# A bidirectional mLSTM and convolution block on one core: projections in another order, and the scan's incoming weights made on ScalarE

## The chip, the core and the metric

The kernel runs on one core of a Trainium2 chip. The core has a matrix engine (TensorE; PE in the views, its weight loads PEld), VectorE (DVE), ScalarE (ACT), GpSimd (POOL) and SyncE (SP, which here only issues DMAs). Each engine works through its own instructions in the order in which the program holds them, and waits on semaphores for the others. The metric is the device time of one execution in microseconds. Before the change it is 2687.62 us, the median of three runs from 2687.34 to 2690.5.

## What is computed

One layer over 2048 latent tokens and 256 context tokens of width 1024. One input projection with 11,296 columns feeds a gated convolution and an mLSTM scan that runs in both directions over 8 heads. Both outputs are projected again, merged with sigmoid gates, projected out and added to the input. Cut to its core:

```python
hx = rmsnorm(x, g_norm[l]) * (1 + scale[:, None, :]) + shift[:, None, :]
px = hx @ w_in[l] + b_in[l]
h_ctx, ctx_states = mlstm_bidir(pc[..., :STATE_COLS], (zero_state(bsz), zero_state(bsz)), not last)
h_x, _ = mlstm_bidir(px[..., :STATE_COLS], ctx_states, True)
out_x = mixer_output(h_x, px[..., STATE_COLS:], True, ...)
x = x + gate[:, None, :] * out_x
# one step of the scan, per chunk
m_row = jnp.maximum(log_w.max(-1), log_inter)
s = jnp.einsum('bhid,bhjd->bhij', qc, kc) * jnp.exp(log_w - m_row[..., None])
w_inter = jnp.exp(log_inter - m_row)
num = jnp.einsum('bhij,bhje->bhie', s, vc) + w_inter[..., None] * jnp.einsum('bhid,bhde->bhie', qc, C)
C_new = decay[..., None, None] * C + jnp.einsum('bhj,bhjd,bhje->bhde', wk, kc, vc)
```

## The kernel before

**Halves and pairs.** The tokens are worked in two halves of 1024. For each half the input projection is cut into 44 "pairs" of 256 columns, named by a letter and a number 0 to 3: k, v, q are the scan's, o and z its output gates, X, C, Z, B the convolution's (X and C are multiplied and convolved, Z is the SiLU path, B the last factor), a and b the merge gates. `pair` (L396 on) makes each product with seven block products instead of eight ("ops" 0 to 6, banks X Y X W Z V Z), each of 12 matmuls of 512 columns (L412), so 84 a pair. The operands are split in a high and a low part: `split` (L177) has ScalarE cast the high part (`wh`, L178) and VectorE subtract the low part (`wl`, L179), which the third matmul of an op reads. `Stream` keeps the weight operands three ops ahead; GpSimd makes their sums (`sw`, L345).

**What follows a pair.** `half_fins` (from L883) holds what is done with a pair's four results. On VectorE three of them first get an addend (L874, or L881 together with the bias); then C costs one multiplication and two shifted multiply-adds each (L942, L947, L949), Z two operations each (L962, L963), z two (L927, L928), B one (L970), and o, a, b none. Bank Z is written by op 4, read by the addend of `fin(1, 1)` on VectorE, and written again by op 6: the matmuls of op 6 wait for that read.

**Side work.** Generators run beside the dense matmuls, some steps for each matmul: `prep_b` and `late_rows` prepare the second half's input and the output weights (1024 columns wide on VectorE, L205, L217, L295, L1289, L1312), `ctx_scan` and `state_scan` carry the states, `scan` makes the outputs. TensorE's order is that of the code (manual schedule). On the other engines a scheduler sets the order when the program is built; `pin` keeps marked instructions in program order there.

**The scan.** For every two chunks `load` (L753) fetches tokens `tk`, queries and keys `qk` and a tile `mw` with the row maxima and the incoming weights of both directions, read from the scratch `mwd` where `gate_finish` (L560) put them (`mr` and `wr`). `mask` (L776) has GpSimd fill the masked part of the maxima. `start` (L784) takes two exponentials on ScalarE (`wt`, L792), the score matmul, two VectorE products (`pt` L796, `qw` L799) and a weighted value tile `vw` (`weigh`, L628) on GpSimd. After it come the state update (L636, L640) and the output matmuls (L842, L843).

**Between the halves.** `xB.load` (L252) fetches the second half's operands into the slots of the first half's, as the last pair lets go of them (slots x0 to x27, four to each op), and splits them; then the gate weights `gw` (L473, L475) are loaded and split.

Of the kernel before, what the change touches and what calls it, by code (L numbers as in the profile page):

```python
# [41 lines left out]
def hybrid_kernel(ctx: ExitStack, tc, x, c, ctxt, c_ctx, w_ada, b_ada, g_norm, w_in, b_in,  # L42
# [425 lines left out]
    mwd = [dp.tile([64, 2, 2, P], F32, name=f"mwd{i}") for i in range(2)]  # L468
# [91 lines left out]
    def gate_finish(key, d, half):  # L560
        g = gt[key][d]
        n, nch = g["n"], g["nch"]
        mp = tp.tile([P, 8, nch], F32, tag="gtmp", name=nm("mp"), bufs=3)
# [17 lines left out]
        g.update(dec=dec, wk=wk)  # L581
# [46 lines left out]
    def weigh(tk, wk):  # L628

        vw = tp.tile([P, 129], F32, tag="vw", name=nm("vw"), bufs=3)  # L630
        pin(nc.gpsimd.tensor_scalar(vw, tk[:, VT], wk, None, op0=OP.mult))  # L631
        return vw
# [111 lines left out]
    def scan(pool, heads, half, done=None):  # L744
# [8 lines left out]
        def load(m):  # L753

            if m >= len(flat) // 2:
                return
# [4 lines left out]
            qks[m] = pool.tile([P, 2, 2, P], F32, tag="qk", name=nm("qk"), bufs=2)
            ld.dma_start(qks[m].rearrange("p a c i -> p a (c i)"), qkd[half][h, :, c0 // 2])
            mws[m] = pool.tile([P, 2, 2, 2, P], F32, tag="mw", name=nm("mw"), bufs=2)
            src = mwd[half]
            ld.dma_start(mws[m], bass.AP(tensor=src.tensor, offset=src.offset + (h * NC + c0) * 4 * P,
                                         ap=[[0, P], [4 * P, 2], [2 * P, 2], [P, 2], [1, P]]))
# [53 lines left out]
        start(0)  # L820
        yield
        due = []
        for n, (h, ch) in enumerate(flat):
            j = h * NC + ch
            if n % 2 == 0:
                load(n // 2 + 1)
            else:
                mask(n // 2 + 1)
# [15 lines left out]
            yield from gap(4)  # L844
# [636 lines left out]
    def begin(m, wait=0):  # L1481
# [4 lines left out]
        xts[m] = []  # L1486
        for i in range(2):
# [96 lines left out]
```

## Time and profile before

| what | us |
|---|---|
| median of the runs | 2687.62 |
| the profiled execution, whole | 2680.46 |
| its span in the trace | 2678.7 |
| TensorE busy | 2602.4 |
| VectorE busy | 1728.2 |
| GpSimd busy | 1151.2 |
| ScalarE busy | 1063.5 |

The profiled execution is one of its own, 7.2 us under the median. The span is what the trace shows; 1.8 us lie around it. A view of stretches of time ("windows") gives for each stretch the busy time of each engine, the granted TensorE clock as a share of full speed, and what the DMAs moved. The timeline lists instructions with their start, their duration and, in brackets, how long the engine stood idle before them and what ended that.

The first half's pairs k0 to v3 end at about 382 us, its other pairs run to about 1057 us, the second half's to about 2070 us, the four branch projections to 2507 us, the output projection to the end.

### The profile page before, as it was taken

The page shows a single profiled execution, that of the slowest core. Times are in us where ns is not written, and L with a number is a line of the kernel's source. Part 1 is how long each engine was busy: PE and PEld are TensorE (multiplying, and loading weights), DVE is VectorE, ACT ScalarE, POOL GpSimd, SP SyncE. Part 2 cuts the span into 40 slices and gives each one's busy share as a digit, 9 for nine tenths or more (in the row PEclk, how much of TensorE's full clock was granted, in tenths as well). Part 3 has the DMA queues.
Part 4 walks back from the last instruction along what each step waited for, and adds up shares of the span by engine and source line. Part 5 has one row for each costly group of instructions (what it writes and reads, how often), then busy time and mean ns, then how long its engine had stood idle before and what let it go on. Part 6 is the DMA issues. An engine that isn't in the chain of part 4 may idle for free.

```text
span 2678.7 us, 38162 instructions
## 1 busy us (share of the span) xinstructions
PE 2602.4 (97%) x12807; PEld 2172.9 (81%) x12807; DVE 1728.2 (65%) x3113; ACT 1063.5 (40%) x2170; POOL 1151.2 (43%) x1371
## 2 busy tenths in 40 slices
PE   7999999999999999999999999999999999999998
PEld 6788887787778887877887888888888888788777
DVE  5643238887876657478578577667666655554697
ACT  4533344333343435343443444344444433332333
POOL 2221223232345443235555564565655235432664
PEclk8999999999999999999999999999999999999999
DMA  7323343454643567424644654653566978868542
GB/s 222 105 92 109 101 150 122 158 180 144 214 145 100 174 178 238 128 91 146 205 151 117 205 159 126 191 174 128 157 193 210 304 238 259 286 195 284 202 164 95
DMA packets 370080, 458.09 MB, mean 171 GB/s; under 512 B 23852, under 2 KB 268252, under 8 KB 369884
## 3 DMA queue, kind: packets, MB, share of 16 engines
q1 hardware_dynamic: 369648, 455.57, 54.3%
q8 instruction: 102, 1.67, 0.3%
q14 instruction: 94, 0.77, 0.1%
q10 hardware_dynamic: 236, 0.08, 0.0%
HBM read 324.60 MB, written 130.97 MB: 170 GB/s over the span
## 4 chain that ended last, share of the span: by engine, by line
PE 82%; DVE 8%; issue 3%; DMA 3%; ACT 2%; POOL 2%; SPq 0%; ACTq 0%; POOLq 0%; DVEq 0%
PE pd L412 58%; PE pd L459 12%; PE pn L842 2%; PE pn L843 2%; PE pc L439 2%; DVE wl L179 2%; PE pn L636 1%; PE pa L647 1%; PE pa L794 1%; PE pu L636 1%; DVE cv L947 1%; PE pd L492 1%; DMA x<-xod 1%; DVE t2k L874 1%; DVE x L179 1%
## 5 line engine op out<-in xcount | busy, mean ns | idle before, releaser
L412 PE MATMUL pd<-x,wh 128*128 128x512 f32 x5320 | 1699.2, 398 | 18.2 <-DVE t2k L874 11.0
L412 PEld LDWEIGHTS pd<-x,wh 128*128 128x128 f32 x5320 | 986.8, 189 | 212.0 <-issue 23.8
L412 PE MATMUL pd<-x,wl 128*128 128x512 f32 x2660 | 1059.6, 398 | 0.0
L412 PEld LDWEIGHTS pd<-x,wl 128*128 128x128 f32 x2660 | 502.8, 189 | 99.3 <-issue 0.2
L178 ACT CAST wh<-sw 128x512 fp32r<-128x512 f32 x384 | 238.0, 620 | 506.2 <-PE pd L412 422.3
L179 DVE TENSOR_TENSOR wl<-sw,wh 128x512 fp32r<-128x512 f32 x384 | 314.9, 821 | 186.6 <-ACT wh L178 180.0
L178 ACT CAST wh<-wr 128x512 fp32r<-128x512 f32 x352 | 217.6, 619 | 404.7 <-PE pd L412 267.6
L345 POOL TENSOR_TENSOR sw<-wr,sw 128x512 f32<-128x512 f32 x96 | 136.5, 1422 | 455.7 <-DVE wl L179 404.0
L179 DVE TENSOR_TENSOR wl<-wr,wh 128x512 fp32r<-128x512 f32 x352 | 287.1, 816 | 47.7 <-ACT wh L178 46.7
L459 PE MATMUL pd<-x,wh 128*128 128x512 f32 x896 | 282.7, 397 | 0.0
L631 POOL TENSOR_SCALAR vw<-tk,wk 128x129 f32<-128x129 f32 x240 | 182.6, 765 | 151.5 <-PE pn L636 119.4
L345 POOL TENSOR_TENSOR sw<-wr 128x512 f32<-128x512 f32 x96 | 131.9, 1374 | 189.1 <-DVE wl L179 182.0
L459 PEld LDWEIGHTS pd<-x,wh 128*128 128x128 f32 x896 | 167.1, 189 | 32.2
L459 PE MATMUL pd<-x,wl 128*128 128x512 f32 x448 | 174.2, 399 | 0.0
L345 POOL TENSOR_TENSOR sw<-sw,wr 128x512 f32<-128x512 f32 x96 | 134.8, 1404 | 70.1 <-DVE wl L179 59.2
L874 DVE TENSOR_TENSOR t2k<-pd,u 128x512 f32<-128x512 f32 x168 | 115.5, 687 | 62.2 <-PE pd L412 60.7
L855 ACT ACTIVATE hf<-pn,rd 128x128 f32<-128x128 f32 x128 | 46.9, 366 | 273.1 <-DVE rd L851 254.3
L780 POOL TENSOR_SCALAR_AFFINE_SELECT mw<-mw 128x256 f32<-128x256 f32 x128 | 62.9, 511 | 205.3 <-DMA mw<-mwd 166.4
L345 POOL TENSOR_TENSOR sw<-wr,wr 128x512 f32<-128x512 f32 x96 | 135.7, 1413 | 17.2 <-DMA wr<-in_w_in_dram 7.8
L186 POOL TENSOR_SCALAR ssq<-ssq 128x1 f32<-128x1 f32 x128 | 36.3, 284 | 198.7 <-ACT hf L857 193.3
L842 PE MATMUL pn<-tk,pt 128*128 128x129 f32 x512 | 98.9, 275 | 4.7 <-DVE hb L856 4.7
L881 DVE SCALAR_TENSOR_TENSOR t2k<-pd,cols,u 128x512 f32<-128x512 f32 x73 | 54.7, 750 | 71.2 <-PE pd L412 68.4
(244 smaller groups left out, 3309.8 us busy)
## 6 DMA issues: line engine op xcount, KB each, us to landing
wr<-in_w_in_dram SPq DMA_DIRECT2D x176, 512.0 KB, 3.8
mw<-mwd SPq DMA_DIRECT2D x64, 512.0 KB, 4.9
tk<-tokd SPq DMA_DIRECT2D x64, 386.0 KB, 3.9
qkd<-t2k SPq DMA_DIRECT2D x64, 256.0 KB, 2.8
qk<-qkd SPq DMA_DIRECT2D x64, 256.0 KB, 4.1
tk<-tokd SPq DMA_DIRECT2D x48, 257.0 KB, 2.8
tokd<-t2k SPq DMA_DIRECT2D x32, 258.0 KB, 3.0
x<-in_w_ada_dram SPq DMA_DIRECT2D x16, 512.0 KB, 6.8
```

Source lines behind the costliest of these rows:

```text
L178: a = nc.scalar.copy(hi, raw)
L179: b = (eng or nc.vector).tensor_tensor(lo, raw, hi.bitcast(F32), op=OP.subtract)
L345: nc.gpsimd.tensor_tensor(s, a, b, op=op)
L412: nc.tensor.matmul(ps[b], op[wi][:, kk, :], xs.at(o, xi, kk), start=(fresh and kk + pi == 0), stop=(o == last[b] and kk == 3 and pi == 2), ...
L439: nc.tensor.matmul(cps[:, s], op[wi][:, kk, :], cx[ci][xi][:, kk, :], start=(first and kk + pi == 0), stop=(not first and kk == 3 and pi = ...
L459: nc.tensor.matmul(pss[j], ops[k // 4][wi][:, k % 4, :], y(xi, k, j), start=(k + pi == 0), stop=(k == NK - 1 and pi == 2))
L631: pin(nc.gpsimd.tensor_scalar(vw, tk[:, VT], wk, None, op0=OP.mult))
L636: nc.tensor.matmul(pu, tk[:, KT], vw, start=True, stop=True)
L780: pin(nc.gpsimd.affine_select(mws[m][:, :, 0, d, :], mws[m][:, :, 0, d, :], pattern=[[0, 2], [s, P]], base=0, channel_multiplier=-s, compa ...
L842: nc.tensor.matmul(pn[:, d, :], pt[:, d, :], tk[:, VT], start=True, stop=False)
L874: nc.vector.tensor_tensor(t, ps, add, op=OP.add)
L881: nc.vector.scalar_tensor_tensor(dst, ps, bcol(col), add, op0=OP.add, op1=OP.add)
```

## The change

Four things are changed: the order of the pairs in both halves, where the weights `wr` and the values `vw` are made, when `mw` and `qk` are fetched, and two small lengths (the wait after a fetch of the last branch's operands, 24 steps instead of 12, and one small tile for two in the output).

```diff
-    mwd = [dp.tile([64, 2, 2, P], F32, name=f"mwd{i}") for i in range(2)]
+    mwd = [dp.tile([64, 2, P], F32, name=f"mwd{i}") for i in range(2)]
...
-        wr = tp.tile([64, P], F32, tag="ar", name=nm("wr"), bufs=1)
-        nc.scalar.activation(wr, mr, AF.Exp, bias=mpc, scale=-1.0)
-        ld.dma_start(mwd[half][:, 0, d, :], mr)
-        ld.dma_start(mwd[half][:, 1, d, :], wr)
+        ld.dma_start(mwd[half][:, d, :], mr)
...
-        vw = tp.tile([P, 129], F32, tag="vw", name=nm("vw"), bufs=3)
-        pin(nc.gpsimd.tensor_scalar(vw, tk[:, VT], wk, None, op0=OP.mult))
+        vw = tp.tile([P, 129], F32, tag="vw", name=nm("vw"), bufs=2)
+        pin(nc.scalar.activation(vw, tk[:, VT], AF.Copy, scale=wk))
...
+        def load_rows(m):
...
+            mws[m] = pool.tile([P, 2, 2, 2, P], F32, tag="mw", name=nm("mw"), bufs=2)
+            src = mwd[half]
+            ld.dma_start(mws[m][:, :, 0], bass.AP(tensor=src.tensor, offset=src.offset + (h * NC + c0) * 2 * P,
+                                                  ap=[[0, P], [2 * P, 2], [P, 2], [1, P]]))
+            qks[m] = pool.tile([P, 2, 2, P], F32, tag="qk", name=nm("qk"), bufs=2)
+            ld.dma_start(qks[m].rearrange("p a c i -> p a (c i)"), qkd[half][h, :, c0 // 2])
...
         def mask(m):
...
+                for ch in sorted((flat[2 * m][1], flat[2 * m + 1][1])):
+                    j = flat[2 * m][0] * NC + ch
+                    for d in range(2):
+                        pin(nc.scalar.activation(mws[m][:, ch % 2, 1, d, :], mws[m][:, ch % 2, 0, d, :], AF.Exp,
+                                                 bias=g[d]["mp"][:, j:j + 1], scale=-1.0))
...
             if n % 2 == 0:
                 load(n // 2 + 1)
-            else:
-                mask(n // 2 + 1)
...
             if n + 1 < len(flat):
                 start(n + 1)
+            if n % 2:
+                load_rows((n + 1) // 2 + 1)
             yield from gap(4)
...
+            if n % 2 == 0:
+                yield
+                mask(n // 2 + 1)
...
-    todo = plan(kinds, "q0 q1 q2 q3 k0 v0 k1 v1 k2 v2 k3 v3 X0 C0 Z0 B0 X1 C1 Z1 B1 X2 C2 Z2 B2 X3 C3 Z3 B3 "
-                       "o0 z0 o1 z1 o2 z2 o3 z3 a0 a1 a2 a3 b0 b1 b2 b3")
+    todo = plan(kinds, "q0 q1 q2 q3 k0 v0 k1 v1 k2 v2 k3 v3 " +
+                " ".join(f"X{r} C{r} a{r} Z{r} b{r} B{r} o{r} z{r}" for r in range(4)))
...
-    heads = [f"k{r} v{r} q{r} o{r} z{r} X{r} C{r} Z{r} B{r}" for r in range(4)]
+    heads = [f"q{r} o{r} z{r} X{r} C{r} {x} Z{r} {y} B{r}"
+             for r, (x, y) in enumerate((("k1", "v1"), ("k2", "v2"), ("k3", "v3"), ("a0", "a1")))]
...
-    todo = plan(kinds, " ".join(heads) + " a0 a1 a2 a3 b0 b1 b2 b3")
+    todo = plan(kinds, "k0 v0 " + " ".join(heads) + " a2 a3 b0 b1 b2 b3")
...
-    urgent.extend(yb.fetch(k) for k in ready)
+    urgent.extend(yb.fetch(k, 24) for k in ready)
```

The change adds lines, so that the program after it has other line numbers: L874 becomes L892, L942 to L949 become L960 to L967, L927 and L928 become L945 and L946, L1289 becomes L1307, L792 becomes L805, L780 becomes L793. The new exponentials are L789.

**VectorE behind a C pair of the first half.** The rows run from the last shifted multiply-add of C to the addend read of bank Z by the pair that follows. Before, that pair is Z3 (`xb` is the side work, `u` the running sums of the pair):

```order
L949 SCALAR_TENSOR_TENSOR cv_6027<-cv_5857,cols_117,cv_6027 128x8x63
L421 TENSOR_TENSOR u_6075<-pd_6058,u_6050 128x512
L179 TENSOR_TENSOR wl_6078<-wr_5880,wh_6077 128x512
L179 TENSOR_TENSOR wl_6102<-sw_6099,wh_6101 128x512
L962 SCALAR_TENSOR_TENSOR t2k_6095<-t2k_6093,t2k_6095 128x512
L1312 TENSOR_TENSOR xb_6066<-xb_6066,xb_5592 128x1024
L963 TENSOR_TENSOR cv_5921<-cv_5921,t2k_6095 128x512
L426 TENSOR_TENSOR u_6122<-pd_6105,u_6075 128x512
L179 TENSOR_TENSOR wl_6125<-wr_5974,wh_6124 128x512
L1312 TENSOR_TENSOR xb_6110<-xb_6110,xb_5592 128x1024
L874 TENSOR_TENSOR t2k_6145<-pd_6128,u_6122 128x512
```

After, the second C pair with the light pair a1 behind it, where the side work is as wide (`acc`):

```order
L967 SCALAR_TENSOR_TENSOR cv_5367<-cv_5196,cols_117,cv_5367 128x8x63
L421 TENSOR_TENSOR u_5414<-pd_5398,u_5390 128x512
L179 TENSOR_TENSOR wl_5417<-wr_5219,wh_5416 128x512
L179 TENSOR_TENSOR wl_5438<-sw_5435,wh_5437 128x512
L1307 SCALAR_TENSOR_TENSOR acc<-xb_5358,sc,acc 128x1024
L426 TENSOR_TENSOR u_5457<-pd_5441,u_5414 128x512
L179 TENSOR_TENSOR wl_5460<-wr_5315,wh_5459 128x512
L892 TENSOR_TENSOR t2k_5476<-pd_5463,u_5457 128x512
```

The two operations of Z (L962, L963) are gone from this stretch, and one wide operation of the side work.

**VectorE between the halves.** Rows with slot numbers: x10 to x27 are operand slots of the second half, `wl` the low parts of its first weights. Before, where the last pair is b3:

```order
L179 TENSOR_TENSOR x10_2229_9581<-x10_2229_9581,x8_2227_9579 128x1024
L179 TENSOR_TENSOR wl_2252_9655<-wr_2249_9650,wh_2251_9654 128x512
L874 TENSOR_TENSOR t2k_2215_9530<-pd_2212_9511,u_2211_9509 128x512
L179 TENSOR_TENSOR x11_2230_9582<-x11_2230_9582,x9_2228_9580 128x1024
L179 TENSOR_TENSOR x14_2233_9585<-x14_2233_9585,x12_2231_9583 128x1024
L874 TENSOR_TENSOR t2k_2217_9547<-pd_2216_9534,u_2211_9509 128x512
L475 CAST gw_2247_9641<-zero_87 128x8x16 x4
L179 TENSOR_TENSOR x15_2234_9586<-x15_2234_9586,x13_2232_9584 128x1024
L874 TENSOR_TENSOR t2k_2218_9563<-pd_2212_9511,u_2198_9456 128x512
L179 TENSOR_TENSOR x18_2237_9589<-x18_2237_9589,x16_2235_9587 128x1024
L179 TENSOR_TENSOR wl_2257_9665<-sw_2255_9662,wh_2256_9664 128x512
```

After, where the last pair is z3 (L946 is its last VectorE operation):

```order
L946 SCALAR_TENSOR_TENSOR cv_2178_9382<-cv_2178_9382,t2k_2216_9556 128x512
L179 TENSOR_TENSOR x22_2240_9590<-x22_2240_9590,x20_2238_9588 128x1024
L179 TENSOR_TENSOR x23_2241_9591<-x23_2241_9591,x21_2239_9589 128x1024
L179 TENSOR_TENSOR x26_2244_9594<-x26_2244_9594,x24_2242_9592 128x1024
L179 TENSOR_TENSOR x27_2245_9595<-x27_2245_9595,x25_2243_9593 128x1024
L475 CAST gw_2246_9638<-zero_87 128x8x16 x4
L179 TENSOR_TENSOR gw_2246_9638<-t2k_2247_9639,gw_2246_9638 128x8x32
L179 TENSOR_TENSOR wl_2251_9652<-wr_2248_9647,wh_2250_9651 128x512
L179 TENSOR_TENSOR wl_2256_9662<-sw_2254_9659,wh_2255_9661 128x512
L179 TENSOR_TENSOR wl_2258_9666<-wr_2249_9649,wh_2257_9665 128x512
```

The low part of the first weights of k0 stood behind the operand in slot x10; now it stands behind the last operand, slot x27, and behind the gate weights.

**ScalarE in the scan.** Before, one chunk's rows with the casts of the dense stream among them:

```order
L855 ACTIVATE hf_15251<-pn_15223,rd_15249 128x128
L178 CAST wh_15236<-wr_14904 128x512
L857 ACTIVATE hf_15251,ssq_14766<-hb_14944 128x128
L792 ACTIVATE wt_15272<-mw_15103,a_10192 128x128
L792 ACTIVATE wt_15272<-mw_15103,a_10199 128x128
L178 CAST wh_15293<-sw_15291 128x512
```

After, a chunk that begins a new tile of maxima:

```order
L872 ACTIVATE hf_13278,ssq_12876<-hb_13060 128x128
L178 CAST wh_13288<-wr_13087 128x512
L789 ACTIVATE mw_13157<-mw_13157,mp_1476 128x128
L789 ACTIVATE mw_13157<-mw_13157,mp_10588 128x128
L789 ACTIVATE mw_13157<-mw_13157,mp_1476 128x128
L789 ACTIVATE mw_13157<-mw_13157,mp_10588 128x128
L805 ACTIVATE wt_13308<-mw_13157,a_1407 128x128
L805 ACTIVATE wt_13308<-mw_13157,a_1414 128x128
L631 ACTIVATE vw_13317<-tk_13217,wk_10610 128x129
L178 CAST wh_13333<-sw_13331 128x512
```

Four exponentials for every two chunks and one weighted value tile for every chunk have come into ScalarE's order between the casts.

More of the change, by code (lines that the diff above doesn't have):

```diff
@@ L562, in gate_finish @@
         n, nch = g["n"], g["nch"]
-        mp = tp.tile([P, 8, nch], F32, tag="gtmp", name=nm("mp"), bufs=3)
+        if half is None:
+            mp = tp.tile([P, 8, nch], F32, tag="gtmp", name=nm("mp"), bufs=3)
+        else:
+            mp = cp.tile([P, 8, nch], F32, name=nm("mp"))
         ml = tp.tile([P, 8, nch], F32, tag="gtmp", name=nm("ml"), bufs=3)
@@ L580, in gate_finish @@
         nc.scalar.activation(wk, wk, AF.Exp)
-        g.update(dec=dec, wk=wk)
+        g.update(dec=dec, wk=wk, mp=mpf)
         if half is None:
@@ L760, in load @@
             ld.dma_start(tks[m], tokd[half][h, :, c0:c0 + 2])
[L761 to L766, printed above, removed]
             if m % 2 == 0:
@@ L774, in load @@
                 ld.dma_start(cur0[h], std[0 if half == 1 else 2][h])
+        def load_rows(m):
+            if m >= len(flat) // 2:
+                return
+            h = flat[2 * m][0]
+            c0 = min(flat[2 * m][1], flat[2 * m + 1][1])
+            mws[m] = pool.tile([P, 2, 2, 2, P], F32, tag="mw", name=nm("mw"), bufs=2)
[4 more added lines that the diff above has]
+            ld.dma_start(qks[m].rearrange("p a c i -> p a (c i)"), qkd[half][h, :, c0 // 2])
         def mask(m):
             if m < len(flat) // 2:
+                for ch in sorted((flat[2 * m][1], flat[2 * m + 1][1])):
[3 more added lines that the diff above has]
+                                                 bias=g[d]["mp"][:, j:j + 1], scale=-1.0))
                 for d in range(2):
@@ L814, in finish @@
                 done(h)
+        load_rows(0)
         load(0)
@@ L820, in scan @@
         start(0)
+        load_rows(1)
         yield
@@ L843, in scan @@
                 nc.tensor.matmul(pn[:, d, :], qw[:, d, :], cur if d == carried else tk[:, ST], start=False, stop=True)
-            yield from gap(4)
+            yield from gap(4 if n % 2 else 3)
             cur = new
@@ L1486, in begin @@
         xts[m] = []
+        sx = so.tile([P, 2, 4], F32, tag="sx", name=nm("sx"), bufs=3)
         for i in range(2):
@@ L1490, in begin @@
             ld.dma_start(xt, x[row:row + P, :])
-            xts[m].append((xt, row, so.tile([P, 4], F32, tag="sx", name=nm("sx"), bufs=6), []))
+            xts[m].append((xt, row, sx[:, i, :], []))
         yield from gap(wait)
```

## The prediction

> **What bounds the kernel now.** I read the page's table of engines first.
>
> ```profile
> span 2678.7 us, 38162 instructions
> PE 2602.4 (97%) x12807; PEld 2172.9 (81%) x12807; DVE 1728.2 (65%) x3113; ACT 1063.5 (40%) x2170; POOL 1151.2 (43%) x1371
> ```
>
> TensorE is busy 97% of the span, and the change neither adds nor takes away a matmul. So all that can move is the time in which TensorE stands still or runs at a lower clock. The windows say where that is (span of the stretch, then PE, PEld, DVE, ACT, POOL, granted clock, DMA):
>
> ```profile
> 382.00:714.00 332.00, 321.18 (x1419) 262.33 (x1419) 269.52 (x349) 124.77 (x214) 106.80 (x88) 0.98 0.51 165
> 714.00:1040.00 326.00, 321.49 (x1484) 264.46 (x1483) 208.13 (x359) 129.48 (x202) 155.29 (x159) 0.99 0.51 157
> 1040.00:1070.00 30.00, 27.04 (x116) 21.74 (x115) 27.08 (x36) 21.45 (x30) 3.17 (x3) 0.94 0.92 285
> 1192.00:2070.00 878.00, 866.57 (x4449) 730.35 (x4448) 611.10 (x1282) 382.27 (x879) 498.50 (x648) 1.00 0.54 164
> 2070.00:2507.00 437.00, 429.56 (x2138) 362.18 (x2137) 230.79 (x475) 139.09 (x326) 172.86 (x238) 1.00 0.80 259
> ```
>
> Length less PE busy is the idle time: 10.8, 4.5, 3.0, 11.4 and 7.4 us. These 37 us, with the clock lost behind some of them, are all that the change can win in these stretches. Stretches that it hardly touches (start, output projection) are left at nothing. The list of TensorE's waits gives the single ones: start, duration, and in brackets the idle time and what ended it.
>
> **Term 1: the order of the first half, 382 to 714 us.**
>
> ```profile
> 464.00 0.71 PE L412 MATMUL pd<-x,wh 128*128 128x512 f32 x2 [1.62 <-DVE t2k L874]
> 527.03 0.70 PE L412 MATMUL pd<-x,wh 128*128 128x512 f32 x2 [1.76 <-DVE t2k L874]
> 606.53 0.70 PE L412 MATMUL pd<-x,wh 128*128 128x512 f32 x2 [2.78 <-DVE t2k L874]
> 689.93 1.19 PE L412 MATMUL pd<-x,wh 128*128 128x512 f32 x2 [3.53 <-DVE t2k L874]
> ```
>
> 9.7 of the 10.8 us stand in four waits, all in the pair behind a C pair: op 6 may not write bank Z before VectorE has read it. VectorE is late with that read because it works off C's tail, then side work and Z's own operations:
>
> ```profile
> 675.91 1.78 DVE L947 SCALAR_TENSOR_TENSOR cv<-cv,cols,cv 128x504 f32<-128x504 f32 x1
> ...
> 683.34 0.68 DVE L962 SCALAR_TENSOR_TENSOR t2k<-t2k,t2k 128x512 f32<-128x512 f32 x1
> 683.94 2.31 DVE L1312 TENSOR_TENSOR xb<-xb,xb 128x1024 f32<-128x1024 f32 x1
> ...
> 687.98 1.21 DVE L1312 TENSOR_TENSOR xb<-xb,xb 128x1024 f32<-128x1024 f32 x1
> 689.11 0.68 DVE L874 TENSOR_TENSOR t2k<-pd,u 128x512 f32<-128x512 f32 x1
> ```
>
> The light pair a or b has none of Z's two operations, 2 x 0.68 = 1.36 us, and in the order shown above one wide side operation less, 1.21 us; together 2.57. Of the four waits that leaves 0, 0, 0.2 and 1.0 us, so 8.5 go. Two of them cost clock as well:
>
> ```profile
> 606.00:612.00 6.00, 5.47 (x17) 4.38 (x18) 5.66 (x9) 4.02 (x6) 0.00 (x0) 0.72 0.29 87
> 690.00:696.00 6.00, 6.00 (x14) 4.69 (x15) 5.65 (x9) 3.75 (x6) 0.00 (x0) 0.50 0.87 294
> 527.00:533.00 6.00, 5.96 (x26) 4.98 (x27) 5.65 (x10) 4.06 (x7) 0.00 (x0) 1.00 0.57 172
> ```
>
> Busy time x (1 - clock) is 1.5 and 3.0 us; behind the wait of 1.76 nothing is lost, so a remainder of 1 us costs none. That is 8.5 + 4.5 = 13.0. Z now stands one pair later, behind a and ahead of b, and its own work may cost a us somewhere: I take **-12**. Bounds: nothing but Z's two operations saved at four places, 4 x 1.36 = -5.4; all idle time and clock of the stretch gone, -15.3.
>
> [...]
>
> **Term 2: 714 to 1040 us.** Idle 4.5 us, and one place of lost clock:
>
> ```profile
> 800.38 0.35 PE L636 MATMUL pn<-vw,tk 128*128 128x129 f32 x1 [2.33 <-DVE cst L638]
> 802.00:806.00 4.00, 4.00 (x14) 3.19 (x13) 1.58 (x3) 0.62 (x1) 0.77 (x2) 0.60 0.52 137
> ```
>
> The clock is 4.00 x 0.40 = 1.6, together 6.1 us. Before, this stretch holds the light pairs o, z, a, b beside the state scan; now it also gets C and Z pairs. Best case -6.1; worst, the waits of the first and third C pair (1.62 + 2.78) come back here, +4. I take **-1**, near nothing, since the C pairs here are followed by light ones as in term 1.
>
> **Term 3: between the halves.**
>
> ```profile
> 1047.48 0.69 PE L636 MATMUL pn<-vw,tk 128*128 128x129 f32 x2 [2.40 <-DVE tk L640]
> 1048.00:1052.00 4.00, 4.00 (x13) 3.14 (x13) 2.68 (x4) 1.02 (x2) 0.00 (x0) 0.63 0.85 232
> 1049.61 0.69 DVE L179 TENSOR_TENSOR wl<-wr,wh 128x512 fp32r<-128x512 f32 x1
> 1057.12 0.39 PE L412 MATMUL pd<-x,wl 128*128 128x512 f32 x1
> 1059.01 1.96 SPq L252 DMA_DIRECT2D x<-xod  x3
> 1061.03 0.43 SPq L473 DMA_DIRECT2D t2k<-in_w_in_dram  x1
> 1068.60 0.40 ACT L178 CAST gw<-t2k 128x256 fp32r<-128x256 f32 x1
> 1070.65 0.41 DVE L179 TENSOR_TENSOR gw<-t2k,gw 128x256 fp32r<-128x256 f32 x1
> ```
>
> k0's third matmul, at 1057.12, reads the low part of k0's first weights. Before, VectorE makes it at 1049.61, 7.5 us ahead. In the order after, that operation stands behind the splits of the last operand slots, which are fetched (1059.01) once the last pair has let go of them, and behind the subtraction of the gate weights, whose DMA goes out behind those. Nothing in the change makes these arrive sooner: the last pair is z3 instead of b3, and it frees its slots in the same steps. So the matmul waits for 1070.65 + 0.41 = 1071.06, then 0.69 for its own operand: 1071.7 - 1057.1 = 14.6 us. With VectorE free, the gate weights' subtraction can follow their cast at 1069.0, and the wait is 13.0. I take 14.0. Clock behind it as behind the waits of 2.3 to 3.5 us, 1.5 to 3.0: 2.2. In return the 0.6 us of small waits in this stretch go, and I give half of the wait at 1047.48 with its clock (2.40 + 1.5): -1.9. Sum **+14** (13.7). Bounds: 13.0 + 1.5 - 0.6 - 3.9 = +10, and 14.6 + 3.0 = +18.
>
> **Term 4: scans beside the second half's pairs, 1192 to 2070 us.** Of 11.4 us idle the longest are:
>
> ```profile
> 1652.36 0.46 PE L842 MATMUL pn<-tk,pt 128*128 128x129 f32 x2 [2.06 <-DVE hb L856]
> 1867.75 0.46 PE L842 MATMUL pn<-tk,pt 128*128 128x129 f32 x2 [2.64 <-DVE hb L856]
> ```
>
> Both come while VectorE works off C's own tail, before any operation of Z; C's tail stays. The other 6.7 us are short waits that a light pair behind C and values ready sooner shorten. I take **-4**; bounds -9 (the 2.64 stays) and +3 (a wait of 2.64 more, as k1 or v1 also has addends).
>
> **Term 5: branch stretch, 2070 to 2507 us.**
>
> ```profile
> 2292.45 0.38 PE L636 MATMUL pu<-vw,tk 128*128 128x129 f32 x1 [1.74 <-POOL vw L631]
> 2327.38 0.45 PE L636 MATMUL pu<-vw,tk 128*128 128x129 f32 x1 [3.87 <-POOL vw L631]
> 2327.00:2332.00 5.00, 4.62 (x15) 3.85 (x16) 1.10 (x3) 0.00 (x0) 0.92 (x2) 0.66 1.09 367
> ```
>
> Here GpSimd makes `vw` behind a mask that waits for `mw`. Now ScalarE makes `vw`, and `mw` is half as large and asked for earlier. 1.74 + 3.87 and the clock, 4.62 x 0.34 = 1.6, are 7.2 of the 9.0 us. I take **-6**; bounds -9 and -2 (only the smaller wait gone).
>
> **Term 6: ScalarE's new work.**
>
> ```profile
> L631 POOL TENSOR_SCALAR vw<-tk,wk 128x129 f32<-128x129 f32 x240 | 182.6, 765 | 151.5 <-PE pn L636 119.4
> L792 ACT ACTIVATE wt<-mw,a x256: 385/387/405, 1240.1 to 2396.8; 128x128 f32<-128x128 f32 x128
> POOL mw L780 <- DMA mw<-mwd: 166.4, 47, 24.3
> ACT wh L178 <- PE pd L412: 689.9, 433, 4.7
> ```
>
> The 256 new exponentials have the shape of `wt`, 0.387 us: 99 us. The `vw` in scan and state update (240 in the page's group) at about the same 0.39 are 94 us more. ScalarE goes from 40% to some 47% of the span. Its casts stand waiting for TensorE 689.9 us over 433 times (third row from ScalarE's own list of waits), since weights are made three ops ahead (an op is 12 matmuls of about 0.23 us, so 8.2 us). A burst of four exponentials, two `wt` and a `vw`, 7 x 0.39 = 2.7 us, is hidden in that. The mask's wait for `mw` (166.4 us over 47 times on GpSimd, 3.5 each, one of them 24.3) moves to ScalarE, with casts queued behind it; 3.5 + 2.7 = 6.2 is still under 8.2. Removed: four exponentials, four DMAs and 183 us on GpSimd, which nothing at the end waits for. I take **+2**; bounds 0, and +8 if each of some 30 tiles slipped by a quarter of a us.
>
> The longer wait after the last branch's fetch and the merged small tile issue the same instructions; nothing.
>
> Sum: -12 - 1 + 14 - 4 - 6 + 2 = **-7 us**: 2680.5 to 2673.5 in the profiled execution. That one is 7.2 us under the median of the runs, so the median goes from 2687.6 to **2680.5**.
>
> **Rivals.**
>
> *C's own tail makes the waits* (slower). If what delays VectorE is C's tail and not Z, as in term 4's two rows, the light pair saves only 5.4 us in term 1, and the second half 1, while the wait between the halves stands in full: -5.4 - 1 + 14 - 1 - 4 + 2 = +5, so 2692. It decides where less than about 7 us of terms 1, 2 and 4 are won. For it: L947 took 1.78 us in C's tail. Against: the four waits end behind Z's operations.
>
> *ScalarE held by `mw`*: masks wait longer than 8 us, casts come late, term 6 is +8 or more: about 2687. Against: 3.5 us a wait.
>
> *The wait between the halves is short.* If the low part is in fact made early, or the fetches of the last slots come sooner, about 4 instead of 14: 2670. This is also the case in which the moved order doesn't do what its rows say. Against: the rows' order on VectorE is fixed.
>
> *VectorE and GpSimd stop each other.* If each `vw` on GpSimd blocks VectorE, taking it off GpSimd frees 183 us for VectorE, and nearly all waits behind VectorE and `vw` in terms 1, 2, 4 and 5 go, 15.3 + 6.1 + 11.4 + 9.0 less about 7: -35 + 14 = -21, so 2667, or 2660 with all 42 us.
>
> ```profile
> 1221.84 1.15 POOL L631 TENSOR_SCALAR vw<-tk,wk 128x129 f32<-128x129 f32 x1
> 1221.87 0.73 DVE L947 SCALAR_TENSOR_TENSOR cv<-cv,cols,cv 128x504 f32<-128x504 f32 x1
> ```
>
> Against: here `vw` was stretched and VectorE's L947 took its short time, 0.73 instead of 1.78.
>
> [...] The two rows agree with a contention, but show GpSimd's `vw`, which had begun 0.03 us earlier, as the one that was lengthened.
>
> **How the numbers follow.** Forecast 0.50, its own range 2673 to 2688; a measurement here tells 0.2%, 5.4 us, from no change, so 0.30 of it is faster (under 2682.2) and 0.20 same. C's tail 0.20, slower. ScalarE held 0.10, same. Short wait 0.12, faster. Engines stopping each other 0.08, faster. Faster 0.30 + 0.12 + 0.08 = 0.50, same 0.30, slower 0.20. From 2665 to 2696 the range holds the forecast, the short wait and most of C's tail, and leaves out about 0.15.
>
> **What would show it.** Term 3: TensorE idle 13 to 15 us at the third matmul of the second half's k0, ended by VectorE's `wl`; without it my largest term is wrong. Term 1: no wait over about 1 us, and full clock, in the first two a pairs. Term 5: no wait of over a us ended by `vw`. Term 6: ScalarE about 190 us busier, its waits for `mw` not followed by waits of TensorE for `wh`. Terms 2 and 4: idle time under 5 and 8 us.

## The result: slower, and the profile after

The kernel after takes 2701.46 us, the median of six runs (2698.22 to 2703.81), against 2687.35 us before: a ratio of 1.0055, with a 95% interval of 1.0045 to 1.0065. Forecast was 2680.5 in a range of 2665 to 2696, so the time lies above the range, and the kernel got slower and not faster.

The page's head after the change:

```profile
span 2696.5 us, 38282 instructions
PE 2606.1 (97%) x12807; PEld 2174.3 (81%) x12807; DVE 1715.6 (64%) x3113; ACT 1224.2 (45%) x2694; POOL 939.5 (35%) x1099
```

ScalarE got 161 us busier (some 190 were forecast) and GpSimd 212 us less busy. TensorE has the same instructions. The windows, moved to where the same stretches now lie:

```profile
382.00:714.00 332.00, 327.98 (x1472) 269.30 (x1471) 249.98 (x326) 138.41 (x235) 111.14 (x91) 1.00 0.55 182
714.00:1040.00 326.00, 315.47 (x1456) 258.92 (x1454) 222.15 (x381) 146.46 (x279) 84.35 (x61) 0.99 0.50 148
1040.00:1084.00 44.00, 29.51 (x117) 23.89 (x118) 30.28 (x43) 22.42 (x32) 6.14 (x5) 0.81 0.59 188
1200.00:2084.00 884.00, 861.55 (x4382) 722.38 (x4381) 597.67 (x1262) 471.60 (x1179) 376.71 (x498) 0.99 0.49 147
2084.00:2520.00 436.00, 434.95 (x2186) 367.84 (x2185) 238.01 (x493) 181.31 (x457) 151.78 (x215) 1.00 0.77 251
```

Length less PE busy is now 4.0, 10.5, 14.5, 22.5 and 1.1 us, against 10.8, 4.5, 3.0, 11.4 and 7.4 before. The first half gained, the branches gained, and two places lost: the one between the halves, and the scans of the second half. Six of the larger waits of TensorE, from its timeline:

```profile
465.01 0.70 PE L412 MATMUL pd<-x,wh 128*128 128x512 f32 x2 [1.84 <-DVE t2k L892]
923.98 0.46 PE L636 MATMUL pn<-vw,tk 128*128 128x129 f32 x2 [2.08 <-DVE tk L640]
1064.24 0.79 PE L412 MATMUL pd<-x,wl 128*128 128x512 f32 x1 [12.52 <-DVE wl L179]
1498.29 0.38 PE L636 MATMUL pu<-vw,tk 128*128 128x129 f32 x1 [3.49 <-ACT vw L631]
1669.74 0.57 PE L857 MATMUL pn<-tk,pt 128*128 128x129 f32 x2 [3.12 <-DVE hb L871]
1891.53 0.50 PE L857 MATMUL pn<-tk,pt 128*128 128x129 f32 x2 [3.69 <-DVE hb L871]
```

The third is the wait that the prediction named. The last three are new or larger: before, there was none at the place of the first of them, and 2.06 and 2.64 us at the places of the other two. ScalarE's own list of waits (us in all, times, longest) and GpSimd's have a row each that is new too:

```profile
ACT wt L805 <- POOL mw L793: 67.4, 75, 3.2
```

```profile
POOL mw L793 <- ACT mw L789: 30.1, 12, 10.6
```

Before, no such row stands among ScalarE's waits. The timeline of all engines ahead of the wait at 1498.29 shows how the two belong together (rows of ScalarE and GpSimd picked out of it):

```profile
1491.14 1.68 POOL L345 TENSOR_TENSOR sw<-wr,sw 128x512 f32<-128x512 f32 x1 [12.45 <-DMA cst<-std]
...
1492.66 1.28 ACT L789 ACTIVATE mw<-mw,mp 128x128 f32<-128x128 f32 x4
1492.89 1.62 POOL L345 TENSOR_TENSOR sw<-wr,wr 128x512 f32<-128x512 f32 x1
...
1495.21 1.58 POOL L345 TENSOR_TENSOR sw<-sw,wr 128x512 f32<-128x512 f32 x1 [0.69 <-DVE wl L179]
1496.74 0.77 POOL L793 TENSOR_SCALAR_AFFINE_SELECT mw<-mw 128x256 f32<-128x256 f32 x2
1497.18 0.76 ACT L805 ACTIVATE wt<-mw,a 128x128 f32<-128x128 f32 x2 [3.24 <-POOL mw L793]
1497.85 0.39 ACT L631 ACTIVATE vw<-tk,wk 128x129 f32<-128x129 f32 x1
```

The four exponentials (L789) read the raw maxima; the mask (L793) overwrites them in place, so it may not start before 1493.9, and in GpSimd's order it stands behind three weight sums (`sw`). The mask comes at 1496.74, when the last of them is through. ScalarE stands 3.24 us at `wt`, with `vw` queued behind it, and TensorE waits for `vw`.

At 1891.53 the mask is a part of the cause, with `hf` queued behind `wt`, and `hb` behind `hf`. `hf` reads `rd`, which VectorE has ready at 1888.90 behind C's tail, and runs at 1890.65, so the wait for the mask costs at most 1.75 of the 3.69 us. At 1669.74 the mask is not in the way; there C's tail alone makes `hb` late, as it did before. The rows of the one and the other:

```profile
1888.75 0.15 DVE L866 RECIPROCAL rd<-den 128x2 f32<-128x2 f32 x1
1890.65 0.35 ACT L870 ACTIVATE hf<-pn,rd 128x128 f32<-128x128 f32 x1
```

```profile
1667.70 1.62 DVE L967 SCALAR_TENSOR_TENSOR cv<-cv,cols,cv 128x504 f32<-128x504 f32 x1
1669.25 0.34 DVE L871 SCALAR_TENSOR_TENSOR hb<-pn,rd,hf 128x128 f32<-128x128 f32 x1
```

### The profile page after: what moved, and what is told of

It is laid out like the page before. It is cut to its first block, busy times and chain, and to the rows that moved or that the text cites. A ratio compares the mean times of both kernels' runs of the same rounds, so it can differ in the third digit from the quotient of the medians.

```text
span 2696.5 us, 38282 instructions
## 1 busy us (share of the span) xinstructions
PE 2606.1 (97%) x12807; PEld 2174.3 (81%) x12807; DVE 1715.6 (64%) x3113; ACT 1224.2 (45%) x2694; POOL 939.5 (35%) x1099
## 4 chain that ended last, share of the span: by engine, by line
PE 44%; DVE 4%; issue 2%; ACT 2%; POOL 2%; DMA 1%; POOLq 0%; DVEq 0%; ACTq 0%
PE pd L412 24%; PE pd L459 13%; PE pn L857 2%; PE pn L858 2%; PE pa L807 1%; PE pu L636 1%; DVE wl L179 1%; POOL sw L345 1%; PE pa L822 0%; PE pn L636 0%; ACT wh L178 0%; ACT wt L805 0%; PE pa L647 0%; POOL ssq L187 0%; DVE t2k L980 0%
## 5 line engine op out<-in xcount | busy, mean ns | idle before, releaser
L412 PE MATMUL pd<-x,wh 128*128 128x512 f32 x5320 | 1698.5, 397 | 14.3 <-DVE xt L1540 7.2
L412 PEld LDWEIGHTS pd<-x,wh 128*128 128x128 f32 x5320 | 987.3, 189 | 209.5 <-issue 15.8
L412 PE MATMUL pd<-x,wl 128*128 128x512 f32 x2660 | 1059.5, 398 | 12.5 <-DVE wl L179 12.5
L412 PEld LDWEIGHTS pd<-x,wl 128*128 128x128 f32 x2660 | 502.7, 189 | 112.6 <-DVE wl L179 12.9
L179 DVE TENSOR_TENSOR wl<-wr,wh 128x512 fp32r<-128x512 f32 x352 | 281.4, 800 | 49.7 <-ACT wh L178 46.4
L459 PE MATMUL pd<-x,wh 128*128 128x512 f32 x896 | 281.3, 395 | 0.0
L459 PEld LDWEIGHTS pd<-x,wh 128*128 128x128 f32 x896 | 166.3, 188 | 31.9
L459 PE MATMUL pd<-x,wl 128*128 128x512 f32 x448 | 173.2, 396 | 0.0
L892 DVE TENSOR_TENSOR t2k<-pd,u 128x512 f32<-128x512 f32 x168 | 115.2, 686 | 61.2 <-PE pd L412 60.1
L805 ACT ACTIVATE wt<-mw,a 128x128 f32<-128x128 f32 x256 | 93.7, 395 | 67.4 <-POOL mw L793 67.4
L809 DVE SCALAR_TENSOR_TENSOR pt<-pa,wt 128x256 f32<-128x256 f32 x128 | 53.9, 421 | 103.8 <-ACT wt L805 97.5
```

The lines of the kernel that those rows point to most:

```text
L179: b = (eng or nc.vector).tensor_tensor(lo, raw, hi.bitcast(F32), op=OP.subtract)
L412: nc.tensor.matmul(ps[b], op[wi][:, kk, :], xs.at(o, xi, kk), start=(fresh and kk + pi == 0), stop=(o == last[b] and kk == 3 and pi == 2), ...
L459: nc.tensor.matmul(pss[j], ops[k // 4][wi][:, k % 4, :], y(xi, k, j), start=(k + pi == 0), stop=(k == NK - 1 and pi == 2))
L805: pin(nc.scalar.activation(wt[:, d, :], mm[:, 0, d, :], AF.Exp, bias=g[d]["a"][:, j:j + 1], scale=-1.0))
L809: nc.vector.scalar_tensor_tensor(pt, sps[:, None, 0:P].to_broadcast([P, 2, P]), QS, wt, op0=OP.mult, op1=OP.mult)
L892: nc.vector.tensor_tensor(t, ps, add, op=OP.add)
```

## The experiments

Twelve runs. Each ratio is against runs of the kernel before that were taken beside it. Beside the medians I use the lengths of stretches between fixed points of TensorE's work, taken from each trace: the copy `u` (L418), which every pair of these stretches has once, marks the pairs, and the branches run from their first matmul (L459) to the first of the output projection. A stretch then holds the same number of pairs in every kernel, and its length holds idle time and lost clock alike. "Half 1" is the second half.

| kernel | median | 16 pairs from X0 | next 15 | 3 between halves | other 42 of half 1 | branches |
|---|---|---|---|---|---|---|
| before | 2687.35 | 331.8 | 317.8 | 70.8 | 985.7 | 415.7 |
| before_again | (one run, 2689.1) | 330.2 | 317.8 | 73.1 | 987.2 | 418.4 |
| after | 2701.46 | 319.9 | 322.6 | 85.7 | 1002.9 | 407.5 |
| order_only | 2694.86 | 321.6 | 319.1 | 85.7 | 985.9 | 416.1 |
| scan_only | 2688.77 | 330.5 | 313.3 | 72.8 | 1003.0 | 407.4 |
| b3_last | 2688.99 | 320.1 | 322.6 | 71.9 | 1005.1 | 407.4 |
| mask_first | 2680.00 | 321.8 | 322.6 | 85.8 | 980.3 | 407.4 |
| burst4 | 2682.93 | 321.7 | 322.6 | 84.6 | 983.2 | 407.4 |
| mask_b3 | 2666.56 | 320.2 | 322.6 | 72.4 | 981.6 | 407.4 |
| mask_b3_vwpool | 2665.94 | 320.1 | 319.1 | 72.4 | 983.0 | 407.4 |
| oz_last | 2660.69 | 322.8 | 316.7 | 73.3 | 983.9 | 407.4 |
| early_rows | 2674.72 | 327.5 | 318.1 | 71.3 | 982.8 | 407.8 |
| oz_early | 2667.67 | 322.3 | 317.6 | 73.9 | 982.2 | 413.7 |
| oz_oldhalf1 | 2665.96 | 320.9 | 316.7 | 71.9 | 986.5 | 407.4 |

Each length comes from one execution, so small differences need care. The 42 pairs have the same program in mask_first, mask_b3 and oz_last and take 980.3, 981.6 and 983.9 us. The 16 pairs have the same order and the same four waits in before and early_rows and take 331.8 and 327.5; there the clock differs: busy time x (1 - clock), over windows of 4 us from 380 to 712, comes to 4.2 us in before and to nothing in early_rows. So in these two long stretches I take nothing under about 4 us as shown by one pair of profiles. The 15 pairs repeat better: the five kernels with the new first half and `vw` on ScalarE all have 322.6.

**The two orders alone, and ScalarE's part alone.** order_only is the kernel before with both new `plan` strings and nothing else; scan_only is the kernel after with both old ones.

> The kernel before with both new orders of pairs and nothing else: masks, incoming weights and weighted values stay where they were. Both theories expect the wait between the halves (12.5 us and 2.5 us of lost clock in the kernel after) and the gain in 382 to 714 us (about -11). Theory M (the second half lost 15 us because ScalarE now stands behind the mask on GpSimd, which itself must wait for ScalarE's new exponentials): the second half's scans lose as little as before, 11 us idle give or take 4, and the time is 2687 + 15 - 11 + 3 = about 2694. Theory O (the second half lost because its new order puts C's tail beside the scan's chunks): the scans idle 20 us or more in spite of the old ScalarE work, the branch stretch keeps its 9 us, and the time is about 2707.

> The kernel after with both old orders of pairs: only ScalarE's new work, the fetches and the small lengths are changed. No wait between the halves and no gain in 382 to 714 us. Theory M: the second half's scans idle some 20 us as in the kernel after (+11, +4 clock), the branch stretch gains 8: about 2687 + 15 - 8 = 2694, and ScalarE stands for the mask (weights wt behind mw of GpSimd) some 60 us. Theory O: the scans idle about 11 us as before, the branch gains 8: about 2679.

order_only: 2694.86 us, ratio 1.0024 (1.0014 to 1.0033), as theory M had it. Its 42 pairs take 985.9 us, as before, and the waits of 2.06 and 2.64 us for `hb` behind C's tail are there unchanged. scan_only: 2688.77, ratio 0.9998 (0.9989 to 1.0008), between the two forecasts, but its stretches decide: the 42 pairs take 1003.0 us with the old order, the same as with the new one, and ScalarE waits for the mask as long as in the kernel after:

```profile
ACT wt L805 <- POOL mw L793: 66.2, 72, 3.2
```

So the 16 us in the second half come with ScalarE's part (here still together with the early fetch), not with the order. scan_only still ends level with before, because the same part gains 10 us in the branches and 4.5 in the 15 pairs beside the state scan.

**The last pair of the first half.** The tail of the plan (the rest left out), with the b pair at its end:

```diff
-... X3 C3 a3 Z3 b3 B3 o3 z3
+... X3 C3 a3 Z3 o3 B3 z3 b3
```

> The kernel after with the last b pair moved to the end of the first half, as it stood before. In its order on VectorE the low part of k0's first weights stands ahead of the operand in slot x11 again. If that place alone made the wait of 12.5 us between the halves, it goes with its lost clock: 2701.5 - 15 = about 2686.5, and no wait over 3 us stands between 1030 and 1080 us. If the wait is the last operands' own late arrival, it stays or turns up at a later matmul of k0, and the time stays within 4 us of 2701.

2688.99 us, ratio 1.0005 (0.9996 to 1.0014), 12.5 us under the kernel after. VectorE's timeline has k0's first `wl` between the operands' splits, as before:

```profile
1046.88 0.69 DVE L179 TENSOR_TENSOR wl<-wr,wh 128x512 fp32r<-128x512 f32 x1
1047.48 1.22 DVE L179 TENSOR_TENSOR x<-x,x 128x1024 fp32r<-128x1024 f32 x1
```

The wait is gone and the three pairs take 71.9 us instead of 85.7. Late operands alone did not make it: in b3_last VectorE splits the last of them only at 1064.94, 10 us after k0's first copy `u` (1054.8), and in the kernel after it was through with all of them at 1062.7. What differs is the place of k0's `wl`, ahead of these splits or behind them:

```profile
1064.94 1.22 DVE L179 TENSOR_TENSOR x<-x,x 128x1024 fp32r<-128x1024 f32 x1
1066.07 0.42 DVE L179 TENSOR_TENSOR gw<-t2k,gw 128x256 fp32r<-128x256 f32 x1
```

**The mask without the exponentials ahead of it.** The raw maxima stay in one half of the tile, the masked ones go to the other, and the weights are made in place once `wt` is taken (lines shortened):

```diff
-                        mws[m][:, :, 0, d, :], mws[m][:, :, 0, d, :], pattern=...
+                        mws[m][:, :, 1, d, :], mws[m][:, :, 0, d, :], pattern=...
...
-                pin(nc.scalar.activation(wt[:, d, :], mm[:, 0, d, :], AF.Exp, bias=..., scale=-1.0))
+                pin(nc.scalar.activation(wt[:, d, :], mm[:, 1, d, :], AF.Exp, bias=..., scale=-1.0))
+            for d in range(2):
+                pin(nc.scalar.activation(mm[:, 0, d, :], mm[:, 0, d, :], AF.Exp, bias=g[d]["mp"][:, j:j + 1], scale=-1.0))
```

> The kernel after with the mask written to the free half of the tile from the raw row maxima, so that it waits for the DMA alone and no longer for ScalarE's exponentials; those are taken in place behind the two wt of each chunk, two for each chunk. The same number of instructions on every engine. Theory M: ScalarE's wait for the mask falls from 67 us to under 25, the second half's scans lose some 8 to 12 us less, about 2691. Theory O: nothing changes by more than 3 us, about 2701.

2680.00 us, ratio 0.9971 (0.996 to 0.9982): 21 us under the kernel after, twice what I expected. Its timeline at the same chunk (GpSimd, then ScalarE):

```profile
1487.30 0.78 POOL L788 TENSOR_SCALAR_AFFINE_SELECT mw<-mw 128x256 f32<-128x256 f32 x2 [11.51 <-DMA tokd<-tk]
```

```profile
1490.83 0.69 ACT L800 ACTIVATE wt<-mw,a 128x128 f32<-128x128 f32 x2
1491.42 0.69 ACT L802 ACTIVATE mw<-mw,mp 128x128 f32<-128x128 f32 x2
1492.00 0.40 ACT L631 ACTIVATE vw<-tk,wk 128x129 f32<-128x129 f32 x1
```

The mask is done 2.8 us before `wt` wants it, ahead of the sums on GpSimd; ScalarE no longer has a wait of `wt` for the mask in its list. The 42 pairs fall from 1002.9 to 980.3 us, 5 to 7 under before. TensorE's idle time in the second half's scans falls from 22.5 us to 8.7, the length less the busy time of this window:

```profile
1202.00:2067.00 865.00, 856.27 (x4393) 721.49 (x4392) 601.92 (x1266) 469.93 (x1183) 384.85 (x505) 1.00 0.52 151
```

The wait at 1891.53 has no counterpart over 1 us here; of the one at 1669.74, which was C's tail, 2.19 us stay.

burst4 puts the four exponentials back in one burst, but behind the first chunk's `wt` and no longer ahead of it (against mask_first, shortened):

```diff
-            for d in range(2):
-                pin(nc.scalar.activation(mm[:, 0, d, :], mm[:, 0, d, :], AF.Exp, ...))
+            if n % 2 == 0:
+                for c2 in sorted((flat[n][1], flat[n + 1][1])):
+                    for d in range(2):
+                        row = mws[n // 2][:, c2 % 2, 0, d, :]
+                        pin(nc.scalar.activation(row, row, AF.Exp, ...))
```

> The kernel with the mask first, but the four exponentials of a tile again in one burst, behind the first chunk's two wt. If the burst of four on ScalarE had been what cost the kernel after its 20 us, it comes back: about 2700. If it was the mask's wait for them (theory M), the time stays within 4 us of 2680 and ScalarE still doesn't wait for the mask.

2682.93 us, ratio 0.998 (0.9969 to 0.9991); the 42 pairs take 983.2. ScalarE still has no wait for the mask. So a burst of four costs little: 2.9 us between the medians, with intervals that overlap. The other 18.5 us go with the rest of the edit, which is the mask's wait for the exponentials and also their 1.3 us on ScalarE ahead of `wt`. No run takes these two apart; in the chunk shown ScalarE lost 3.24 us to the one and 1.28 to the other.

**Both mended, and what `vw` is worth.** mask_b3 holds both edits; mask_b3_vwpool also has `vw` on GpSimd again.

> The kernel after with both edits, the mask first and b3 last. If the two losses are apart from each other the gains add: 2680.0 - 12.5 = about 2667.5, 0.8% under the kernel before. If one feeds the other (the wait between the halves shifts the scans against the pairs), it is 2672 or more.

> The same with the weighted values back on GpSimd (two buffers as in the kernel after). If moving them to ScalarE won the branch stretch, its waits of TensorE for vw come back (5.6 us and 1.6 of clock before): 2667.5 + 7 = about 2675. If the mask, which no longer waits for a late DMA in front of them on GpSimd, had been the cause there, no such wait over 1 us comes back and the time is within 3 us of 2667.5; the two waits of 2.1 us in 915 to 970 us then shrink to 1.1 as in the run with the orders alone.

mask_b3: 2666.56, ratio 0.9919 (0.9905 to 0.9934). The gains add, so neither loss feeds the other by more than the scatter of the runs. mask_b3_vwpool: 2665.94, ratio 0.9916 (0.9899 to 0.9933): the same. Its branches take 407.4 us, with TensorE never idle in this window:

```profile
2066.00:2500.00 434.00, 434.00 (x2171) 367.00 (x2170) 228.78 (x478) 165.50 (x409) 171.11 (x238) 1.00 0.80 256
```

So moving `vw` did not win the branch stretch. The two waits beside the state scan shrink as expected, to 1.04 us at 923.91 and 1.13 at 964.30. In order_only, with the old fetch, the wait stands as before:

```profile
2332.95 0.80 PE L636 MATMUL pu<-vw,tk 128*128 128x129 f32 x2 [4.89 <-POOL vw L631]
```

**The early fetch alone.** early_rows is the kernel before with `load_rows`, the earlier `mask`, the two small lengths and two buffers for `vw` instead of three; `wr` comes by DMA and `vw` from GpSimd, in the old orders (shortened):

```diff
-            mws[m] = ... 
-            ld.dma_start(mws[m], ...)
...
+            if n % 2:
+                load_rows((n + 1) // 2 + 1)
...
+            if n % 2 == 0:
+                yield
+                mask(n // 2 + 1)
```

> The kernel before with only the early fetch and the early mask of the change (rows and queries asked for one tile sooner, mask one step sooner) and its small lengths; both halves of the tile come by DMA as before, weighted values on GpSimd, both old orders. If the early fetch is what won the branch stretch, its waits for vw (5.6 us and 1.6 of clock) go without any new work on ScalarE: 2688 - 8 = about 2680, and the scans idle about 11 us as before. If the halved transfer or ScalarE's part was needed, the waits stay and the time is within 3 us of 2688.

2674.72 us, ratio 0.9959 (0.9943 to 0.9975). That is 5 us under the forecast of 2680. The branches take 407.8 us without any new work on ScalarE, so that stretch was won by the fetch and mask a step earlier or by the small lengths, which no run takes apart. The longer wait after a fetch acts in this stretch: the last branch's operands (`x` from `ybd`) are asked for from 2307 us on in the kernel before, around its wait at 2327.38. The gain is also a narrow one. The mask still stands behind its DMA in early_rows, and `vw`, 3.7 us behind it, is done at 2316.70 for a matmul that runs at 2316.75:

```profile
2312.42 0.78 POOL L791 TENSOR_SCALAR_AFFINE_SELECT mw<-mw 128x256 f32<-128x256 f32 x2 [8.51 <-DMA mw<-mwd]
```

**Which orders are worth keeping.** oz_last is mask_first with `X{r} C{r} a{r} Z{r} b{r} B{r}` in the first half and o, z and the last b at its end; oz_oldhalf1 is the same with the old second half; oz_early has the orders of oz_last with the rows of early_rows.

> The mask first, and the first half with the light pair behind each C as after, but o and z kept for the end beside the state scan as before, b3 last. If the waits of 2 to 3 us between 770 and 1045 us come from C and Z pairs standing beside the state scan, they go: 2667.5 - 5 = about 2662. If the state scan makes them by itself with whatever pair, 2667 to 2668. If the denser C pairs early bring waits back behind C, 2670 or more.

> The mask first, the first half's order with o and z kept for the end and b3 last, but the old order of the second half. If the second half's order is worth nothing, as the equal idle times of the scans with either order say (22.4 and 22.4 us), it is 2660.7 within 3 us; if a light pair behind C is worth the 4 us that the prediction gave it, 2665.

> The early fetch and mask with both halves of the tile by DMA and the weighted values on GpSimd, the first half's order with o and z kept for the end and b3 last, the second half's new order. No new work on ScalarE at all. If ScalarE's exponentials buy nothing, it is within 3 us of the run with the mask first in the same order (2660.7). If the halved transfer counts, it is 2664 or more.

oz_last: 2660.69, ratio 0.99 (0.9882 to 0.9918), the fastest median of all, 1.0% under before; its interval overlaps that of mask_b3. The 15 pairs beside the state scan fall from 322.6 to 316.7 us, and the waits of 2.1 to 2.3 us between 770 and 970 us are gone, so they came with the C and Z pairs there. The profiled execution of oz_last was the slowest of its four (2666.08), and its five stretches add up to 2104.1 us, as much as those of mask_b3 (2104.2), so the profiles don't show the gain in the whole. oz_oldhalf1: 2665.96 (0.9907 to 0.994), 5.3 us above oz_last, and the intervals overlap. Its 42 pairs are 2.6 us longer, less than the scatter, and its five stretches together 0.7 us shorter, so what the second half's order is worth is not shown. oz_early: 2667.67 (0.9917 to 0.9944), 7 us above oz_last. In its profile the branches are 6.3 us longer, mostly by one wait for `vw` on GpSimd and the clock behind it (0.79 from 2316 to 2324, with TensorE busy 7.09 us: 1.5 us); that execution was the slowest of its six (2673.67), so the others may not have had the wait:

```profile
2316.91 0.62 PE L639 MATMUL pu<-vw,tk 128*128 128x129 f32 x2 [3.50 <-POOL vw L634]
```

early_rows and mask_b3_vwpool, also with `vw` on GpSimd, have no such wait in their branches. Whether the halved transfer is what keeps it away is not settled.

**The kernel before once more.**

> The kernel before, unchanged, for a second profile: the first one's execution was 7 to 8 us under the median of the runs. If single waits come and go from run to run, this one shows 5 to 8 us more idle or half-clocked time, in places that wait for a DMA; if the difference is even, all stretches are longer by a third of a per cent.

2689.1 us, span 2687.4, 8.7 longer than the first profile. TensorE's waits come to 72.1 us in all beside 68.3, in the same places, and TensorE is busy 2607.3 beside 2602.4 with the same instructions, at a mean granted clock of 0.990 beside 0.992: the other 4.9 us are clock. So both readings held in part, and the first profile caught an execution some 8 us short. The waits for `vw` here are these:

```profile
2296.61 0.80 PE L636 MATMUL pu<-vw,tk 128*128 128x129 f32 x2 [3.53 <-POOL vw L631]
...
2332.40 0.54 PE L636 MATMUL pu<-vw,tk 128*128 128x129 f32 x2 [2.22 <-POOL vw L631]
```

## Why the prediction was wrong, step by step

The steps against the stretches of the table, after less the mean of the two profiles of before. The measured ones add up to +14.2, and the medians differ by 14.1:

| term | forecast | measured |
|---|---|---|
| 1, the first half's order | -12 | 319.9 - 331.0 = -11.1 |
| 2, the 15 pairs beside the state scan | -1 | 322.6 - 317.8 = +4.8 |
| 3, between the halves | +14 | 85.7 - 72.0 = +13.7 |
| 4 and 6, the second half's scans and ScalarE | -4 + 2 | 1002.9 - 986.5 = +16.4 |
| 5, the branches | -6 | 407.5 - 417.1 = -9.6 |

**Term 3 was right** in place and size. The wait of 12.5 us stands at the matmul that the prediction named, with 2.6 us of lost clock behind it (from 1064 to 1072 TensorE is busy 7.76 us at 0.67). b3_last removes both; there the clock is 1.00 from 1040 to 1084.

**Term 1 was right in size, and in place at three of four waits.** The first of the four, at 464.00, did not stand in the pair behind C. Its rows before show pair B0 (L970), with Z's last operation, at 451.83, long done, and VectorE held by side work (L205) that waits for GpSimd:

```profile
457.28 0.75 DVE L970 SCALAR_TENSOR_TENSOR cv<-pd,cols,cv 128x512 f32<-128x512 f32 x1
...
461.90 0.75 DVE L205 TENSOR_SCALAR xb<-xb,rs 128x1024 f32<-128x1024 f32 x1 [1.86 <-POOL rs L187]
462.57 0.69 DVE L179 TENSOR_TENSOR wl<-wr,wh 128x512 fp32r<-128x512 f32 x1
463.17 0.68 DVE L874 TENSOR_TENSOR t2k<-pd,u 128x512 f32<-128x512 f32 x1
```

The new order could not remove it, and it is there after, 1.84 us at 465.01. So idle time fell by 6.8 us and not by 8.5. Of the other 4.3 of the 11.1, some 3.5 are clock: over the windows of 4 us from 380 to 712 the two profiles of before lose 4.2 and 2.9 us, and the kernel after nothing. The new order can't claim all of that: early_rows, in the old order, has the same four waits, loses no clock there, and its stretch is 3.5 us shorter than before.

**Term 6 failed, and with it the sign.** The step was: "A burst of four exponentials, two `wt` and a `vw` ... is hidden", and "The mask's wait for `mw` ... moves to ScalarE". It counted ScalarE's time and a wait for the DMA. ScalarE never waited for that DMA (no idle time stands before the 256 exponentials, L789). What I left out is that the exponentials read the very rows that GpSimd's mask overwrites. That makes a way from ScalarE to GpSimd and back where there had been one from DMA to GpSimd to ScalarE, and GpSimd's turn can come behind three sums of 1.6 us, as at the two places above. ScalarE stood 67.4 us in it, over 75 waits; its stretch lost 16.4 us against before, 22.6 against mask_first, which has as many instructions on every engine. The weights' lead of 8.2 us, on which the cover rested, was an estimate: three ops of 12 matmuls at some 0.23 us, as 321.18 us over 1419 in the window from 382 to 714 has it. For the casts the cover held, as no wait of a pair's matmul (L412) for `wh` stands in TensorE's list after. For `hf` and `vw`, which the scan's matmuls wait for within a chunk, it did not: TensorE's waits for `hb` (which reads `hf`) and `vw` in the scans are 8.8 and 4.7 us, and 2.8 and 1.1 in mask_first. The copy `u` on ScalarE came late too, 3.2 us over four waits, and none of these stands in mask_first. Against the forecast of -2 for terms 4 and 6 this is 18.4 of the 21 us by which the whole was missed.

**Term 4 is not shown.** Four pairs of kernels differ by the second half's order within the same scan. With the new order the 42 pairs are 0.6 us shorter (order_only beside before), 0.6 (oz_early beside early_rows), 0.1 (after beside scan_only) and 2.6 (oz_last beside oz_oldhalf1). That is short of the -4, also where no mask is in the way. What the term said of the two long waits, that C's tail makes them and they stay, held.

**Term 2 was mis-signed.** The worst case of the text (+4) is what came. C's tail and Z's operations now stand beside the state scan, and its `tk` (L640) comes late behind them, at 923.50 behind L965 of 1.77 us and at 964.87 behind L980 of 1.79; with o and z there instead, the stretch is 5.9 us shorter. About 3.5 of it depend on `vw` standing on ScalarE as well (322.6 and 319.1, both in after beside order_only and in the two mended kernels): the waits at 923.98 and 965.36 are 2.08 and 2.10 us with it, and 1.05 and 1.12 in order_only. In the old order `vw` on ScalarE does no such harm (313.3 in scan_only, 317.8 before). Why the two act together stays open.

**Term 5 had the sign and, in the main, the wrong cause.** It won more than forecast. I put it to `vw` leaving GpSimd and, in half a sentence, to the earlier fetch. With `vw` back on GpSimd nothing returns; with the early fetch and mask and the small lengths it is won, without new work on ScalarE. I had put the small lengths at nothing, which no run tests by itself.

None of the rivals was this. "ScalarE held by `mw`" had the right engine and the right tile, but the DMA as the cause and +8 as its price. The slower rival, C's own tail, fell in the first half, where term 1 won most of what it could; in the second half C's tail kept its waits, as that rival has it.

## What to carry to other kernels

When an operation goes to another engine, list who else reads and writes the same rows: here an operation in place on a third engine turned that into a hop, and its price was what was queued there, three sums of 1.6 us at the two places shown, and not its own 0.4 us. Writing the mask's result beside its input, with the exponentials behind `wt`, was worth 21 us here and added no instruction on any engine. Where operands are fetched again as the last block lets go of them, look at what stands behind them on the engine that splits them. And the two profiles of the kernel before differ by 4.9 us in TensorE's busy time with the same instructions (granted clock 0.992 and 0.990), so compare stretches between fixed points, and take the profile twice.

## What the hardware showed that I had not expected

**The same wait cost clock in one execution and none in another.** In the second profile of the kernel before, a wait of 1.31 us at 1151.72 is followed by this window (the clock, 0.61, is the third figure from the end). In the first profile the same wait is 1.30 us, at 1150.86, and the clock from 1152 to 1156 is 1.00. In the same first profile the wait of 2.64 us at 1867.75 cost none: from 1868 to 1872 the clock is 1.00.

```profile
1152.00:1156.00 4.00, 4.00 (x12) 3.16 (x12) 2.91 (x13) 2.12 (x6) 0.00 (x0) 0.61 0.16 47
```

Busy time x (1 - clock) is 1.6 us in this window. So the length of a wait alone doesn't settle the clock behind it, and the prediction's step from nothing lost behind 1.76 us to nothing lost behind 1 us is not safe. What decides it, no run shows.

**A short copy on VectorE grew sixfold beside a sum on GpSimd.** The state scan's copy of 0.22 us (the median of 48 in the kernel after; the longest takes 1.29), in its usual and in its stretched form, the latter with GpSimd's row:

```profile
1038.54 0.22 DVE L728 COPY tk<-cst 128x129 f32<-128x129 f32 x1
```

```profile
921.25 1.58 POOL L345 TENSOR_TENSOR sw<-sw,wr 128x512 f32<-128x512 f32 x1
921.63 1.29 DVE L728 COPY tk<-cst 128x129 f32<-128x129 f32 x1
```

It began 0.38 us after the sum and ended 0.09 after it, 1.29 us in all, on the way to the wait of 2.08 us at 923.98. In order_only the same copy takes 1.32 us beside the same sum, and the wait behind it is 1.05 us, so the copy alone does not set the length of that wait.
